# S5's VectorE work behind both RWKV inverses, an uninterrupted substitution, and the inverse's small products in turn through four quadrants

## The chip, the cores and the metric

The kernel runs on one core of a Trainium2 chip. The metric is the device time of one execution in microseconds. A core has a matrix engine (TensorE, PE in the profile; its weight loads are listed apart as PEld), VectorE (DVE), ScalarE (ACT) and GpSimd (POOL), and SyncE (SP), which here mostly issues DMAs. Each engine works through its own queue in order and waits on semaphores for the others.

## What is computed

Two layers act on 256 latent and 256 context tokens of width 1024. In each layer a gated feed-forward half step is followed by three token mixers on one normalised input, a merge through per-channel gates, and a second feed-forward half step. Cut to the part that matters:

```python
def hybrid_mixer(h, hc, need_ctx_out, w_in, ...):
    proj = h @ w_in; proj_c = hc @ w_in          # u | k | v | f (RWKV) | q | gate columns
    y_s5, y_s5_c = s5_mixer(u_c, u_l, ...)        # complex scans over tokens, both directions, then GELU and a gate
    y_att, y_att_c = gqa_mixer(q_c, k_c, v_c, q_l, k_l, v_l, ...)   # 8 query heads, 2 key heads of 64
    y_rw, y_rw_c = rwkv7_mixer(f_c, f_l, ...)     # 4 heads of 64, both directions
    g_s5, g_att, g_rw = jnp.split(jax.nn.sigmoid(gate_pre), 3, axis=-1)
    mixed = g_s5*(y_s5 @ w_br_s5) + g_att*(y_att @ w_br_att) + g_rw*(y_rw @ w_br_rwkv)
    return mixed @ w_out

def rwkv7_scan(s0, decay, neg_kk, kk_a, v, k, r):   # one step for each token
    sa = einsum(s, nkk_t)
    s = s*w_t + sa*b_t + v_t*k_t
    y = einsum(s, r_t)
```

The last layer gives no output for the context.

## The kernel before

All matmuls of the projections are split into a high and a low part of the weights (`wsplit`, ScalarE copies, VectorE or GpSimd subtracts: tiles gh.. and gl.., wh and wl) and run as three products (L922 to L924). In `mixers` (L1245) the projections come first; then RWKV, S5, attention and the merge share the rest of the stage. The gate projection (24 column blocks, tiles pg) depends on nothing in the mixers, and stands wherever TensorE would otherwise have nothing to do.

RWKV's token recurrence is worked off in chunks of 64 tokens, 4 chunks for each half of 256 tokens (`hf`=0 context, `hf`=1 latent), two directions, four heads. `head` and `piece` (L168 to L222) prepare a half: VectorE builds decayed keys and queries, TensorE multiplies them (tile it, L208), and VectorE masks the results into AM and ZL (L213, L214). Each chunk then needs the inverse of a unit triangular 64x64 matrix. `solve_a` writes the four 16x16 diagonal blocks of all 16 matrices through DRAM (Ad, L233) into a layout with matrices on partitions (G, L235), and inverts them by forward substitution on VectorE: 15 steps of one product (L240) and one sum (L241). The result goes through DRAM back (Sd, L242; D, L246). `solve_b` completes the inverse from 16 to 32 and then to 64: a transposition T (L252) and four batches of small products, pv (L256, 64 products on 16 rows), pS (L261, 64 on 32 rows), pw (L268, 32) and pT (L275, 32). Each product uses one quadrant of the 128 x 128 array, and a batch finishes one quadrant before it starts on the next. `loop` (L279) then carries the state through the chunks.

S5 (`s5_main`, L659 to L738) runs eight group-direction blocks: a product (tile s5v), VectorE products (L687, L688), scans (L694) and a product (L700), GpSimd sums between them, and a product back (tile s5y, L705 and L710). Its end is GELU and a gate (L723 to L737). Attention's pool is opened after S5's is closed and takes its memory, so attention begins (atz, L768, on GpSimd) when S5 is through. An attention unit (`core`, L838; four units in layer 0, two in layer 1) takes 256 or 512 keys: the scores' maxima (tile ats, L849), and then for each of two head groups and each 128 keys a step of three products (tile atp, L869 to L871), Exp on ScalarE (L873, tile atP, one buffer), a copy (L875, atph), a subtraction on VectorE (L876, atpl) and three products (tile ato, L878 to L880). A reciprocal (L884), a product (L885) and a split (L1278, L1279) end a unit. The merge follows: pb..e for S5 and RWKV, pb for attention.

The order of instructions on every engine is set by a scheduler when the kernel is built: it runs its own estimate of each engine's timeline and takes, among what is ready, the instruction written first, where `high_priority` moves a block ahead. `issue_after(i)` is a rule for that scheduler: what the block puts on the engine of instruction i stays behind i in that engine's queue. It is no wait by itself. `Rwkv.run` sets the sequence in which all of this is written:

```python
h0=s.head(0,0); h1=s.head(0,1); s.prep(h0)
between()
s.prep(h1); s.solve_a(0)
h0=s.head(1,0); h1=s.head(1,1); s.prep(h0)
s.solve_b(0); s.prep(h1); s.solve_a(1)
```

Of the kernel before, what the change touches and what calls it, by code (L numbers as in the profile page):

```python
# [52 lines left out]
class Rwkv:  # L53
# [170 lines left out]
    def solve_a(s,hf):  # L224

        K=s.K; nc=K.nc; L=s.L; V=nc.vector; ac=(0,64); nm=f"{L}{hf}"
        Ad=K.dram.tile([64,2,16,64],F32,name=f"Ad{nm}",tag="Ad",bufs=2)
        Sd=K.dram.tile([4,2,16,16,16],F32,name=f"Sd{nm}",tag="Sd",bufs=2)
        AMv=s.AM[:,hf].rearrange("p a c n -> p (a c) n")
        G=s.g1([128,16,16],f"G{nm}"); S=s.g1([128,16,16],f"S{nm}"); s.D=s.g2([128,16,32],f"D{nm}")  # L230
        nc.gpsimd.memset(S,0.0); nc.gpsimd.memset(S.rearrange('p a b -> p (a b)')[:,0:256:17],1.0); nc.gpsimd.memset(s.D,0.0)
        for par in range(2):
            nc.sync.dma_start(Ad[:,par],AMv[par*64:par*64+64,:,ac[par]:ac[par]+64])  # L233
        for b in range(4):
            nc.sync.dma_start(G[b*32:b*32+32],Ad[b*16:b*16+16,:,:,b*16:b*16+16].rearrange("i r s t -> (r s) i t"))  # L235
        tmp=K.rw.tile([128,64],F32,name=f"stmp{nm}",tag="stmp",bufs=1)
        for j in range(15):
            a=j+1; b=15-j
            tv=tmp[:,0:a*b].rearrange("p (a b) -> p a b",a=a)
            V.tensor_mul(tv,S[:,0:a,j:j+1].to_broadcast([128,a,b]),G[:,j:j+1,j+1:16].to_broadcast([128,a,b]))  # L240
            V.tensor_add(S[:,0:a,j+1:16],S[:,0:a,j+1:16],tv)  # L241
        nc.sync.dma_start(Sd.rearrange("b r s i t -> (b r s) i t"),S)  # L242
        for par in range(2):
            for b in range(4):
                r=par*64+b*16
                nc.sync.dma_start(s.D[r:r+16,:,b%2*16:b%2*16+16],Sd[b,par].rearrange("s i t -> i s t"))  # L246

    def solve_b(s,hf):

        K=s.K; nc=K.nc; L=s.L; V=nc.vector; ac=(0,64); nm=f"{L}{hf}"  # L250
        AMv=s.AM[:,hf].rearrange("p a c n -> p (a c) n"); D=s.D
        T=s.g2([128,16,32],f"T0{nm}"); V.transpose(T,D)  # L252
        pv=K.pc([128,16,32],f"pv{nm}")
        for g in range(4):
            R=slice(g*32,g*32+32); H=slice(g*32,g*32+16); c=ac[g//2]+g%2*32
            for m in range(16): h=nc.tensor.matmul(pv[R,m,:],AMv[H,m,c:c+32],T[H,m,:],start=True,stop=True)  # L256
        s.hops.append(h); VT=T; nc.scalar.activation(VT,pv,AF.Copy,scale=K.half[:,1:2])
        pS=K.pc([128,16,32],f"pS{nm}")
        for g in range(4):
            R=slice(g*32,g*32+32)  # L260
            for m in range(16): h=nc.tensor.matmul(pS[R,m,:],VT[R,m,:],D[R,m,:],start=True,stop=True)  # L261
        s.hops.append(h)
        V.tensor_add(D,D,pS)
        V.transpose(T,D)
        pv=K.pc([128,16,32],f"pw{nm}")
        for par in range(2):
            R=slice(par*64,par*64+32); R2=slice(par*64+32,par*64+64); a0=ac[par]
            for m in range(16): h=nc.tensor.matmul(pv[R2,m,:],AMv[R,m,a0+32:a0+64],T[R,m,:],start=True,stop=True)  # L268
            nc.scalar.activation(VT[R2],pv[R2],AF.Copy)
            nc.scalar.activation(AMv[R,:,a0:a0+32],D[R],AF.Copy)  # L270
            nc.scalar.activation(AMv[R2,:,a0+32:a0+64],D[R2],AF.Copy)
        s.hops.append(h); pS=K.pc([128,16,32],f"pT{nm}")
        for par in range(2):
            R=slice(par*64,par*64+32); R2=slice(par*64+32,par*64+64); a0=ac[par]
            for m in range(16): h=nc.tensor.matmul(pS[R,m,:],VT[R2,m,:],D[R2,m,:],start=True,stop=True)  # L275
            V.tensor_copy(AMv[R,:,a0+32:a0+64],pS[R])
        s.hops.append(h)

# [67 lines left out]
    def run(s,between):  # L346
        h0=s.head(0,0); h1=s.head(0,1); s.prep(h0)
        between()
        s.prep(h1); s.solve_a(0)
        h0=s.head(1,0); h1=s.head(1,1); s.prep(h0)  # L350
        s.solve_b(0); s.prep(h1); s.solve_a(1)
        l0=s.loop(0); l1=s.loop(1)
        for _ in range(3): next(l0)
        s.solve_b(1); next(l0); Y0=s.Y if not s.last else None
        for _ in range(4): next(l1)
        if not s.last: s.finish(0,Y0)
        s.finish(1,s.Y)
# [541 lines left out]
D=1024; NF=22; DEPTH=2  # L899
# [343 lines left out]
def ix(v,L): return v[L] if isinstance(v,tuple) else v['v']  # L1243

def mixers(tc,K,L,last):  # L1245
    nc=K.nc; I=K.I; n0=256 if last else 0
# [11 lines left out]
    with tc.tile_pool(name="mc",bufs=1) as mc, tc.tile_pool(name="q0",bufs=1) as q0, tc.tile_pool(name="prm",bufs=1) as K.prm, \  # L1258
# [24 lines left out]
        rw=Rwkv(K,L,W,last); rw.emit=lambda hf,o: ysplit(6,8,o) if last else nc.sync.dma_start(K.yd[:,6:8,hf*256:hf*256+256],o)  # L1283
# [46 lines left out]
        def between():  # L1330
            for o in K.SEQ[b+1:]: op(o)
        rw.run(between)
        with tc.tile_pool(name="s5",bufs=1) as sp, tc.high_priority(offset=ix(K.HS,L)):
            for _ in s5_main(K,L,sp,lambda m,o: ysplit(m,m+1,o.unsqueeze(1)) if last else nc.sync.dma_start(K.yd[:,m],o),last): pass
        N=512-n0; T=lambda sh,n,tag,b,dt=F32: K.rw.tile(sh,dt,name=f"{n}{L}",tag=tag,bufs=b)
        if not last: ay=T([128,2,4,512],"ay","BT",1,F32R)
# [116 lines left out]
```

## Time and profile before

| | |
|---|---|
| median of three runs | 2347.73 us (2344.19 to 2353.74) |
| profiled execution | 2359.33 us, span 2357.6 us |
| mean granted TensorE clock | 0.953 of full speed |
| busy: PE / PEld / DVE / ACT / POOL | 95 / 82 / 69 / 41 / 26% |
| mixers of layer 0, from RWKV's preparation to the end of the gates | 490 to 926 us |
| the same of layer 1 | 1778 to 2116 us |

The page gives shares over the whole span; stages with different limits are mixed in it. The views that cut the span into windows show the busy time of each engine and the granted clock for one stage. Matmuls are pipelined, so that records overlap: a single record lasts longer than the time until the next one starts, and the step of a row of equal matmuls is its length, less the tail of the last, divided by the number of steps.

### The profile page before, as it was taken

What the parts mean: (1) busy time and instruction counts of PE and PEld (TensorE: products, weight loads), DVE (VectorE), ACT (ScalarE), POOL (GpSimd) and SP (SyncE); (2) the same over time, 40 slices, a digit from 0 to 9 for tenths busy, and PEclk for the clock granted to TensorE, in tenths of its full rate; (3) what the DMA queues carried; (4) which work ended last, traced back from release to release, by engine and by line L of the source; (5) the groups of instructions that cost most, each with busy time, mean ns of one, the idle gap of its engine ahead of it and who ended that gap; (6) DMA issues with size and microseconds to landing.
All of it is one profiled execution on the core that took longest, in us unless ns stands there. A gap on an engine that the chain in (4) does not pass through costs nothing.

```text
span 2357.6 us, 40039 instructions
## 1 busy us (share of the span) xinstructions
PE 2242.8 (95%) x14438; PEld 1929.4 (82%) x14438; DVE 1623.2 (69%) x3202; ACT 973.7 (41%) x2005; POOL 607.1 (26%) x726
## 2 busy tenths in 40 slices
PE   7999889988999999899999999999999899998999
PEld 3888668866789889788888888888887688888999
DVE  7895889588855677886457575546557965687655
ACT  4333333433344544443233344334334325565554
POOL 5016660155422233600000002513013533331000
PEclk8999989998869999999999999999999877999999
DMA  7575566334422454545445436546424542365664
GB/s 254 165 225 171 182 214 219 121 119 144 123 82 76 138 163 143 185 141 184 123 143 182 126 131 206 171 155 215 138 65 131 150 126 85 94 194 184 178 188 130
DMA packets 222715, 363.40 MB, mean 154 GB/s; under 512 B 53554, under 2 KB 93618, under 8 KB 222388
## 3 DMA queue, kind: packets, MB, share of 16 engines
q1 hardware_dynamic: 220500, 360.09, 48.3%
q8 instruction: 113, 1.85, 0.3%
q10 hardware_dynamic: 2016, 0.76, 0.1%
q14 instruction: 86, 0.70, 0.1%
HBM read 320.90 MB, written 39.86 MB: 153 GB/s over the span
## 4 chain that ended last, share of the span: by engine, by line
PE 79%; DVE 10%; issue 4%; DMA 3%; POOL 2%; ACT 1%; SPq 1%; DVEq 0%; ACTq 0%; POOLq 0%
PE p L922 17%; PE p L924 17%; PE p L923 16%; PE pg L924 3%; PE pg L922 3%; PE pg L923 3%; DVE s L995 1%; PE pS L261 1%; PE pv L256 1%; PE pq L923 1%; PE po L922 1%; PE po L924 1%; PE po L923 1%; PE pq L922 1%; PE it L208 1%
## 5 line engine op out<-in xcount | busy, mean ns | idle before, releaser
L917 ACT ACTIVATE wh<-wr 128x512 fp32r<-128x512 f32 (+1 forms) x568 | 348.1, 619 | 666.3 <-PE p L923 578.1
L918 DVE TENSOR_TENSOR wl<-wr,wh 128x512 fp32r<-128x512 f32 (+1 forms) x568 | 407.3, 721 | 306.3 <-ACT wh L917 275.1
L922 PE MATMUL p<-hhi,wh 128*128 128x512 f32 (+1 forms) x1440 | 516.6, 363 | 4.7 <-ACT wh L917 3.6
L923 PE MATMUL p<-hlo,wh 128*128 128x512 f32 (+1 forms) x1440 | 518.6, 361 | 1.5 <-DVE hlo L1104 0.9
L924 PE MATMUL p<-hhi,wl 128*128 128x512 f32 (+1 forms) x1440 | 518.6, 361 | 0.6 <-DVE wl L918 0.6
L922 PEld LDWEIGHTS p<-hhi,wh 128*128 128x128 f32 x1440 | 273.2, 191 | 46.7 <-ACT wh L917 4.3
L923 PEld LDWEIGHTS p<-hlo,wh 128*128 128x128 f32 x1440 | 274.2, 190 | 42.9 <-DVE hlo L1104 1.8
L924 PEld LDWEIGHTS p<-hhi,wl 128*128 128x128 f32 x1440 | 274.0, 190 | 42.4 <-DVE wl L918 1.4
L995 DVE SCALAR_TENSOR_TENSOR s<-ad,cb 128x1024 f32<-128x1024 f32 x224 | 286.3, 1280 | 2.9
L924 PE MATMUL p<-ghi,wl 128*128 128x512 f32 (+1 forms) x704 | 248.3, 353 | 0.0
L922 PE MATMUL p<-ghi,wh 128*128 128x512 f32 (+1 forms) x704 | 248.0, 353 | 0.0
L923 PE MATMUL p<-glo,wh 128*128 128x512 f32 (+1 forms) x704 | 247.9, 353 | 0.0
L924 PE MATMUL pg<-hhi,glpg 128*128 128x256 f32 x512 | 157.9, 309 | 11.0 <-DVE glpg L907 9.0
L922 PE MATMUL pg<-hhi,ghpg 128*128 128x256 f32 x512 | 155.5, 304 | 0.3 <-ACT ghpg L906 0.3
L923 PE MATMUL pg<-hlo,ghpg 128*128 128x256 f32 x512 | 152.0, 297 | 0.0
L924 PEld LDWEIGHTS p<-ghi,wl 128*128 128x128 f32 x704 | 133.0, 189 | 18.2 <-issue 0.2
L923 PEld LDWEIGHTS p<-glo,wh 128*128 128x128 f32 x704 | 133.0, 189 | 18.1
L922 PEld LDWEIGHTS p<-ghi,wh 128*128 128x128 f32 x704 | 133.0, 189 | 17.9
L906 ACT ACTIVATE ghpg<-wrpg 128x256 fp32r<-128x256 f32 x176 | 72.3, 414 | 125.3 <-PE pg L923 102.9
L924 PEld LDWEIGHTS pg<-hhi,glpg 128*128 128x128 f32 x512 | 104.6, 205 | 18.8 <-DVE glpg L907 10.9
L907 POOL TENSOR_TENSOR glpg<-wrpg,ghpg 128x256 fp32r<-128x256 f32 x88 | 70.8, 808 | 180.8 <-ACT ghpg L906 168.7
L922 PEld LDWEIGHTS pg<-hhi,ghpg 128*128 128x128 f32 x512 | 104.8, 205 | 6.3 <-ACT ghpg L906 0.5
(722 smaller groups left out, 4325.5 us busy)
## 6 DMA issues: line engine op xcount, KB each, us to landing
wr<-w SPq DMA_DIRECT2D x480, 256.0 KB
ad<-w_ada SPq DMA_DIRECT2D x138, 512.0 KB
wrpg<-w_g SPq DMA_DIRECT2D x96, 256.0 KB
wr<-w SPq DMA_DIRECT2D x64, 192.0 KB
s5tab<-s5tabd SPq DMA_DIRECT2D x16, 640.0 KB
s5tabd<-s5tb SPq DMA_DIRECT2D x16, 384.0 KB
wrpf<-w_f SPq DMA_DIRECT2D x24, 256.0 KB
gd<-gt SPq DMA_DIRECT2D x24, 256.0 KB
```

What stands on the lines that cost most here:

```text
L208: nc.tensor.matmul(pi[:,c,:],BK[R,c].rearrange("p j b -> p (j b)"),s.ZL[par][R,hf,dq,c,o],start=True,stop=True)
L256: for m in range(16): h=nc.tensor.matmul(pv[R,m,:],AMv[H,m,c:c+32],T[H,m,:],start=True,stop=True)
L261: for m in range(16): h=nc.tensor.matmul(pS[R,m,:],VT[R,m,:],D[R,m,:],start=True,stop=True)
L906: K.nc.scalar.activation(hi,raw,AF.Copy)
L907: (K.nc.gpsimd if eng=='pool' else K.nc.vector).tensor_sub(lo,raw,hi.bitcast(F32))
L917: nc.scalar.activation(hi[:,0:n],raw,AF.Copy)
L918: (nc.gpsimd if eng=='pool' or i<=K.PW else nc.vector).tensor_sub(lo[:,0:n],raw,hi[:,0:n].bitcast(F32))
L922: nc.tensor.matmul(ps,lhi,rhi,start=start,stop=False)
L923: nc.tensor.matmul(ps,lhi,rlo,start=False,stop=False)
L924: return nc.tensor.matmul(ps,llo,rhi,start=False,stop=stop).ins
L995: nc.vector.scalar_tensor_tensor(j,raw,1.0,K.cb[:,v,:],op0=ALU.mult,op1=ALU.mult,accum_out=K.M[L][:,v,ct:ct+1])
```

## The change

It has three parts. `solve_a` remembers its last sum (`s.lasts`). After the first half's `solve_a`, one piece of the second half is written freely; the other one, the completion of the first inverse and the second direction's pieces are written under `issue_after(s.lasts)`: VectorE's rows of these come behind the whole first substitution. All of S5 is written under `issue_after(rw.after)`, the last sum of the second substitution. And the loops of the four product batches are exchanged: the matrix index is now the outer loop and the quadrant the inner one, so that successive products go to different quadrants (four of them in pv and pS, two in pw and pT); the copies behind pw get a loop of their own. No arithmetic is added or removed.

```diff
             V.tensor_mul(tv,S[:,0:a,j:j+1]...,G[:,j:j+1,j+1:16]...)
-            V.tensor_add(S[:,0:a,j+1:16],S[:,0:a,j+1:16],tv)
+            s.lasts=V.tensor_add(S[:,0:a,j+1:16],S[:,0:a,j+1:16],tv).ins
...
         pv=K.pc([128,16,32],f"pv{nm}")
-        for g in range(4):
-            R=slice(g*32,g*32+32); H=slice(g*32,g*32+16); c=ac[g//2]+g%2*32
-            for m in range(16): h=nc.tensor.matmul(pv[R,m,:],AMv[H,m,c:c+32],T[H,m,:],start=True,stop=True)
+        for m in range(16):
+            for g in range(4):
+                R=slice(g*32,g*32+32); H=slice(g*32,g*32+16); c=ac[g//2]+g%2*32
+                h=nc.tensor.matmul(pv[R,m,:],AMv[H,m,c:c+32],T[H,m,:],start=True,stop=True)
...
         pv=K.pc([128,16,32],f"pw{nm}")
+        for m in range(16):
+            for par in range(2):
+                R=slice(par*64,par*64+32); R2=slice(par*64+32,par*64+64); a0=ac[par]
+                h=nc.tensor.matmul(pv[R2,m,:],AMv[R,m,a0+32:a0+64],T[R,m,:],start=True,stop=True)
         for par in range(2):
             R=slice(par*64,par*64+32); R2=slice(par*64+32,par*64+64); a0=ac[par]
-            for m in range(16): h=nc.tensor.matmul(pv[R2,m,:],AMv[R,m,a0+32:a0+64],T[R,m,:],start=True,stop=True)
             nc.scalar.activation(VT[R2],pv[R2],AF.Copy)
...
-        h0=s.head(1,0); h1=s.head(1,1); s.prep(h0)
-        s.solve_b(0); s.prep(h1); s.solve_a(1)
+        h0=s.head(1,0); h1=s.head(1,1); s.piece(*h0[:2],0,h0[2][0],h0[3][0])
+        with s.K.tc.issue_after(s.lasts):
+            s.piece(*h0[:2],1,h0[2][1],h0[3][1])
+            s.solve_b(0); s.prep(h1)
+        s.solve_a(1); s.after=s.lasts
...
-        with tc.tile_pool(name="s5",bufs=1) as sp, tc.high_priority(offset=ix(K.HS,L)):
+        with tc.tile_pool(name="s5",bufs=1) as sp, tc.high_priority(offset=ix(K.HS,L)), tc.issue_after(rw.after):
```

pS and pT are turned round in the same way as pv and pw. The change adds 11 lines, all above S5, so that a line of S5, of attention or of the weight split has a number in the changed kernel that is 11 higher (L687 is L698, L880 is L891).

What the scheduler makes of it shows in three places. On VectorE in layer 0, at the first substitution (S, stmp and G are its tiles; th, T, ZL and BK belong to RWKV's preparation, s5.. to S5, and gl.. are split weights). Before:

```order
L240 TENSOR_TENSOR stmp_5684<-S_5673,G_5672 128x15
L169 SCALAR_TENSOR_TENSOR th_5742<-c_rst_4013,th_5742 128x256
L700 TENSOR_TENSOR s5qb_7230<-s5w_7223,s5tab_7209 128x4x127
L241 TENSOR_TENSOR S_5673<-S_5673,stmp_5684 128x15
L907 TENSOR_TENSOR glpg_4933<-wrpg_4930,ghpg_4932 128x256
L168 TENSOR_SCALAR th_5748<-th_5748 128x256
L240 TENSOR_TENSOR stmp_5684<-S_5673,G_5672 128x28
L169 SCALAR_TENSOR_TENSOR th_5748<-c_rst_4013,th_5748 128x256
L182 TENSOR_TENSOR T_5762<-k_4162,u_5754 128x256
L241 TENSOR_TENSOR S_5673<-S_5673,stmp_5684 128x2x14
L187 TENSOR_TENSOR ZL_4032<-kkn_4176,E_5756 64x4x64
```

and now:

```order
L240 TENSOR_TENSOR stmp_5684<-S_5673,G_5672 128x15
L918 TENSOR_TENSOR glkv_4916<-wrkv_4903,ghkv_4915 128x256
L241 TENSOR_TENSOR S_5673<-S_5673,stmp_5684 128x15
L240 TENSOR_TENSOR stmp_5684<-S_5673,G_5672 128x28
L241 TENSOR_TENSOR S_5673<-S_5673,stmp_5684 128x2x14
L918 TENSOR_TENSOR glpg_4933<-wrpg_4930,ghpg_4932 128x256
L240 TENSOR_TENSOR stmp_5684<-S_5673,G_5672 128x39
L241 TENSOR_TENSOR S_5673<-S_5673,stmp_5684 128x3x13
L240 TENSOR_TENSOR stmp_5684<-S_5673,G_5672 128x48
L918 TENSOR_TENSOR glpg_4949<-wrpg_4930,ghpg_4948 128x256
L241 TENSOR_TENSOR S_5673<-S_5673,stmp_5684 128x4x12
```

Between one product of the substitution and its sum stood pieces and S5 rows; now only splits of weights stand among the first steps. In the same queue, at the end of the second substitution of layer 0, before (att.. and at.. rows belong to attention's keys, glq to weights of its queries; S5's last row L737 stood some 50 rows earlier):

```order
L240 TENSOR_TENSOR stmp_6147<-S_6136,G_6135 128x28
L812 TENSOR_TENSOR atvl_7296<-atqw_7318,atvh_7295 128x2x64 x2
L241 TENSOR_TENSOR S_6136<-S_6136,stmp_6147 128x14x2
L791 TENSOR_REDUCE atss_7325<-atsqk_7324 128x4
L240 TENSOR_TENSOR stmp_6147<-S_6136,G_6135 128x15
L907 TENSOR_TENSOR glq_5344<-wrq_5331,ghq_5343 128x256
L792 TENSOR_SCALAR atss_7325<-atss_7325 128x4
L241 TENSOR_TENSOR S_6136<-S_6136,stmp_6147 128x15
```

and now:

```order
L241 TENSOR_TENSOR S_6136<-S_6136,stmp_6147 128x14x2
L325 COPY XV_6189<-p_6264 64x256
L240 TENSOR_TENSOR stmp_6147<-S_6136,G_6135 128x15
L241 TENSOR_TENSOR S_6136<-S_6136,stmp_6147 128x15
L698 TENSOR_TENSOR s5ra_6992<-s5v_6987,s5tab_6983 128x512
L699 TENSOR_TENSOR s5rb_6993<-s5v_6987,s5tab_6983 128x512
L918 TENSOR_TENSOR glq_5480<-wrq_5467,ghq_5479 128x256
```

S5's first VectorE row follows directly on the last sum; before, attention's preparation had come up to this place. On TensorE in layer 0, among the steps of attention's last unit (atq_, atk.., atm and atsel are its queries, keys and maxima, atph and atpl the two parts of the exponentials, pg gates). Before:

```order
L880 MATMUL ato_7865<-atpl_7873,atvh_7295 128x512
L922 MATMUL pg_9121<-hhi,ghpg_9158 128x256
L923 MATMUL pg_9121<-hlo,ghpg_9158 128x256
L924 MATMUL pg_9121<-hhi,glpg_9159 128x256
L922 MATMUL pg_9121<-hhi,ghpg_9158 128x256
L923 MATMUL pg_9121<-hlo,ghpg_9158 128x256
L869 MATMUL atp_7905<-atqs_7661,atkh_7293 128x512
L870 MATMUL atp_7905<-atqs_7661,atkl_7294 128x512
L871 MATMUL atp_7905<-atmT_7300,atsel_7305 128x512
```

and now:

```order
L889 MATMUL ato_7865<-atph_7872,atvh_7295 128x512
L890 MATMUL ato_7865<-atph_7872,atvl_7296 128x512
L891 MATMUL ato_7865<-atpl_7873,atvh_7295 128x512
L880 MATMUL atp_7905<-atqs_7661,atkh_7293 128x512
L881 MATMUL atp_7905<-atqs_7661,atkl_7294 128x512
L882 MATMUL atp_7905<-atmT_7300,atsel_7305 128x512
L889 MATMUL ato_7865<-atph_7885,atvh_7295 128x512
L890 MATMUL ato_7865<-atph_7885,atvl_7296 128x512
L891 MATMUL ato_7865<-atpl_7886,atvh_7295 128x512
```

Between the products of one step stood gate matmuls (and merge products of S5 and RWKV); now one step follows the other, and no gate is left behind them in this layer. In layer 1 it is the same for both units.

## Rows read from the trace of the kernel before

**Rows 1.** The page: PE's busy time, and the granted clock in 40 slices.

```profile
PE 2242.8 (95%) x14438; PEld 1929.4 (82%) x14438; DVE 1623.2 (69%) x3202; ACT 973.7 (41%) x2005; POOL 607.1 (26%) x726
...
PEclk8999989998869999999999999999999877999999
```

**Rows 2.** Busy time by stage, layer 0; columns as in the first line.

```profile
core 0: us, PE busy (x) PEld busy (x) DVE busy (x) ACT busy (x) POOL busy (x), PEclk, DMA share, GB/s
490.00:642.00 152.00, 130.41 (x769) 106.56 (x768) 135.34 (x264) 57.52 (x127) 81.00 (x101) 0.91 0.41 121
642.00:684.00 42.00, 42.00 (x435) 37.49 (x432) 16.47 (x52) 15.17 (x36) 8.12 (x11) 0.51 0.32 88
684.00:926.00 242.00, 241.66 (x2424) 220.52 (x2423) 156.79 (x311) 123.54 (x260) 69.49 (x71) 0.99 0.40 128
```

**Rows 3.** The same view of layer 1.

```profile
1778.00:1920.00 142.00, 120.59 (x744) 103.14 (x743) 124.50 (x263) 56.40 (x135) 64.63 (x91) 0.87 0.47 134
1920.00:2012.00 92.00, 90.69 (x1180) 80.85 (x1177) 46.20 (x105) 39.20 (x94) 29.69 (x37) 0.72 0.28 84
2012.00:2116.00 104.00, 99.58 (x893) 89.32 (x892) 76.61 (x145) 65.12 (x148) 31.57 (x37) 0.98 0.50 152
```

**Rows 4.** VectorE by line, 490 to 642 us (busy us, mean ns | idle before).

```profile
L694 DVE TENSOR_TENSOR_SCAN s5w<-s5m4m,s5ra 128x128 f32<-128x128 f32 x29 | 11.0, 431 | 1.1 <-POOL s5ra L689 1.1
...
L700 DVE TENSOR_TENSOR s5qb<-s5w,s5tab 128x508 f32<-128x508 f32 x8 | 5.9, 742 | 1.7 <-DMA Yd<-s5ysb 1.7
```

**Rows 5.** PE by line, 640 to 756 us: the four product batches.

```profile
L261 PE MATMUL pS<-D,T 32*32 32x32 f32 x256 | 11.5, 215 | 0.0
L256 PE MATMUL pv<-T,AM 16*32 16x32 f32 x256 | 10.9, 208 | 0.8 <-DVE T L252 0.8
L268 PE MATMUL pw<-T,AM 32*32 32x32 f32 x128 | 6.4, 214 | 0.0
L275 PE MATMUL pT<-D,T 32*32 32x32 f32 x128 | 5.9, 203 | 0.0
```

**Rows 6.** The largest of them in layer 1, 1915 to 2012 us.

```profile
L261 PE MATMUL pS<-D,T 32*32 32x32 f32 x256 | 14.2, 237 | 0.0
```

**Rows 7.** PE in order of time (start us, us); last: only 687.20 to 687.21 us.

```profile
724.02 3.93 PE L256 MATMUL pv<-T,AM 16*32 16x32 f32 x128
...
644.22 1.22 PE L256 MATMUL pv<-T,AM 16*32 16x32 f32 x19
...
690.52 0.68 PE L315 MATMUL p<-Z,AM 64*64 64x64 f32 x14
...
687.19 0.69 PE L295 MATMUL p<-XV,ZL 128*64 128x64 f32 x16
...
687.19 0.28 PE L295 MATMUL p<-XV,ZL 128*64 128x64 f32 x2
```

**Rows 8.** Who waited for S5's output tile s5o (us, times).

```profile
  POOL atz L768: 35.2, 2
```

**Rows 9.** PE by line, 904 to 926 us.

```profile
L923 PE MATMUL pg<-hlo,wppg 128*128 128x256 f32 x55 | 15.4, 279 | 0.0
```

**Rows 10.** ScalarE in order of time; last: all Exps of 2076 to 2102 us.

```profile
811.21 0.60 ACT L873 ACTIVATE atP<-atp 128x512 f32<-128x512 f32 x1 [0.51 <-PE atp L871]
811.84 0.63 ACT L875 ACTIVATE atph<-atP 128x512 fp32r<-128x512 f32 x1
...
813.24 0.60 ACT L873 ACTIVATE atP<-atp 128x512 f32<-128x512 f32 x1 [0.45 <-DVE atpl L876]
...
L873 ACT ACTIVATE atP<-atp x8: 578/588/604, 2077.1 to 2101.2; 128x512 f32<-128x512 f32 x8
```

**Rows 11.** VectorE in order of time, 899 to 912 us.

```profile
899.94 0.69 DVE L876 TENSOR_TENSOR atpl<-atP,atph 128x512 fp32r<-128x512 f32 x1 [1.98 <-ACT atph L875]
905.05 3.35 DVE L884 RECIPROCAL atdn<-atdn 128x512 f32<-128x512 f32 x1 [4.42 <-ACT atdn L883]
...
911.13 0.69 DVE L1279 TENSOR_TENSOR ay<-aty,ay 128x512 fp32r<-128x512 f32 x1 [0.58 <-ACT ay L1278]
```

More of the change, by code (lines that the diff above doesn't have):

```diff
@@ L253, in solve_b @@
         pv=K.pc([128,16,32],f"pv{nm}")
-        for g in range(4):
-            R=slice(g*32,g*32+32); H=slice(g*32,g*32+16); c=ac[g//2]+g%2*32
-            for m in range(16): h=nc.tensor.matmul(pv[R,m,:],AMv[H,m,c:c+32],T[H,m,:],start=True,stop=True)
+        for m in range(16):
+            for g in range(4):
+                R=slice(g*32,g*32+32); H=slice(g*32,g*32+16); c=ac[g//2]+g%2*32
+                h=nc.tensor.matmul(pv[R,m,:],AMv[H,m,c:c+32],T[H,m,:],start=True,stop=True)
         s.hops.append(h); VT=T; nc.scalar.activation(VT,pv,AF.Copy,scale=K.half[:,1:2])
         pS=K.pc([128,16,32],f"pS{nm}")
-        for g in range(4):
-            R=slice(g*32,g*32+32)
-            for m in range(16): h=nc.tensor.matmul(pS[R,m,:],VT[R,m,:],D[R,m,:],start=True,stop=True)
+        for m in range(16):
+            for g in range(4):
+                R=slice(g*32,g*32+32)
+                h=nc.tensor.matmul(pS[R,m,:],VT[R,m,:],D[R,m,:],start=True,stop=True)
         s.hops.append(h)
@@ L265, in solve_b @@
         pv=K.pc([128,16,32],f"pw{nm}")
+        for m in range(16):
+            for par in range(2):
+                R=slice(par*64,par*64+32); R2=slice(par*64+32,par*64+64); a0=ac[par]
+                h=nc.tensor.matmul(pv[R2,m,:],AMv[R,m,a0+32:a0+64],T[R,m,:],start=True,stop=True)
         for par in range(2):
             R=slice(par*64,par*64+32); R2=slice(par*64+32,par*64+64); a0=ac[par]
[L268 removed]
             nc.scalar.activation(VT[R2],pv[R2],AF.Copy)
@@ L272, in solve_b @@
         s.hops.append(h); pS=K.pc([128,16,32],f"pT{nm}")
+        for m in range(16):
+            for par in range(2):
+                R=slice(par*64,par*64+32); R2=slice(par*64+32,par*64+64)
+                h=nc.tensor.matmul(pS[R,m,:],VT[R2,m,:],D[R2,m,:],start=True,stop=True)
         for par in range(2):
-            R=slice(par*64,par*64+32); R2=slice(par*64+32,par*64+64); a0=ac[par]
-            for m in range(16): h=nc.tensor.matmul(pS[R,m,:],VT[R2,m,:],D[R2,m,:],start=True,stop=True)
+            R=slice(par*64,par*64+32); a0=ac[par]
             V.tensor_copy(AMv[R,:,a0+32:a0+64],pS[R])
```

## The prediction, made before the changed kernel was run

> **What bounds the kernel now.** I read the page first: TensorE is busy over nearly the whole span [rows 1]. A shorter time must therefore come out of the gaps of TensorE, out of stretches in which its clock is granted at the lower of its two levels (1.2 instead of 2.4 GHz), or out of matmuls that occupy it without need. The slices of the granted clock dip twice, in both layers inside the mixers, so I cut the mixers into stages [rows 2, 3]. Before the RWKV inverse can start ("preparation", 490 to 642 us in layer 0, 1778 to 1920 us in layer 1) TensorE works 130.4 of 152.0 us and 120.6 of 142.0 us. That is 21.6 and 21.4 us of idling, with VectorE busy for 135.3 and 124.5 us of it: VectorE is the engine that is full there. In the stage of the inverses TensorE hardly idles, but the clock is low: 0.51 of full speed over 42 us in layer 0, 0.72 over 92 us in layer 1. Up to the end of attention there is no slack worth naming: 0.3 us of 242 in layer 0, 4.4 us of 104 in layer 1. So the same work could gain in the preparation, in the clock, and in the small products of the inverse. Whatever empties the stage behind them can lose.
>
> **S5 out of the preparation.** By adding up, along VectorE's order, the traced durations of all rows from the first one that differs to the first transposition T of the inverse, 134 us of work stand ahead of T in layer 0 before the change, and 86 us after it (116 and 77 us in layer 1). S5's rows are 34 us of the 134, the scans (11.0 us in this stage) and the products of L700 (5.9) the largest groups [rows 4]; the other 14 are rows that the planner now puts behind T. TensorE has 93 us of work ahead of T in the new order of layer 0, so now the two engines are nearly level, and TensorE is the later one. Of the 21 us of idling I let 9 go in each layer. The bounds are 0 (the chain from one VectorE row to a product and back stays as long as it is) and 21 (all of it). Most of it stays because the substitution has a wait that the change leaves alone: the matrix goes through DRAM to be re-laid. S5's own matmuls are not removed; they are done later, where TensorE had no gap, and so the gap that they filled counts against the 21. S5's DMAs move too: in SP's order the later five of the eight tables and all its writes now stand behind the second substitution's transfers. That frees the substitution's transfers of them, and costs S5 nothing that TensorE sees as long as gate matmuls are left to run. **Sum: −9 and −9.**
>
> **The small products.** Per layer two inverses issue 768 records (384 products, two records each). The busy times of these four groups in layer 0 add to 11.5 + 10.9 + 6.4 + 5.9 = 34.7 us [rows 5]; in layer 1 the largest is 14.2 us and the four make 37.0 [rows 6]. Of one quadrant 128 records took 3.93 us; without the 0.19 us that the last outlives the others, 127 steps make 29.5 ns each at the full clock. At the lower clock 19 took 1.22 us, some 54 ns a step. The row that shows a turn between two quadrants is the loop's L295: its weights have 64 columns, twice as many, and 16 records still take only 0.69 us, some 31 ns each; of these, two had already started in the first 20 ns [rows 7]. So a turn through two quadrants halves the price, and I take that for pw and pT (12.3 to 6 us). Four in turn are not shown. Between the half that two give and the quarter that a perfect overlap would give I take a third for pv and pS: 22.4 to 8 us in layer 0, 25.2 to 9 in layer 1. **Sum: −20 and −22.** Bounds: all at half, −17 and −18; pv and pS at a quarter, −23 and −25; nothing at all, if four quadrants wait for each other. The separate loop of copies behind pw starts the first copies some 16 products later, under half a microsecond per inverse, which other matmuls cover.
>
> The Trainium skill, TensorE: Matmul & The Clock Gate, section "Wait — 56ns, not 53.3ns?", says that starts of matmuls never come closer than about 25 ns, however small they are. By that alone the 768 records would keep 19 us a layer, the gain would be some 27 us in place of 42, and the sum below 15 us higher. The row of L295 speaks against it: two of its records started within 20 ns [rows 7].
>
> **The clock.** In 642 to 684 us half of 42 us is lost, 20.6 us; in layer 1's stretch 0.28 of 92, 25.8 us [rows 2, 3]. Both spells follow a stretch in which TensorE waited, and consist of the small products. With fewer gaps ahead and shorter products some of it must return, but the products still fill only a corner of the array. I take **−8 and −8**, with bounds 0 and −21 and −26 (all of it).
>
> **What is late next: attention.** Attention's first instruction waits for the memory that S5 releases (atz, 35.2 us over the two layers) [rows 8]; S5 ended near 628 us in layer 0, and now can only begin behind the second substitution. TensorE has gate matmuls for that time, but they are the same ones that used to fill attention's steps. In TensorE's new order none is left for the last two attention units of either layer: their steps stand there bare. Before, attention's last result was followed by 22 us of gates in layer 0, of which the last kind alone, 55 of each of three, is 15.4 us a group [rows 9]; they hid everything at its end.
>
> A bare step of one head and 128 keys is a ring: Exp 0.60 us, copy 0.63 us (ScalarE), subtraction 0.69 us (VectorE), and only then the next Exp, since the tile between has one buffer: the Exp waits for atpl. The closest two Exps lie 813.24 − 811.21 = 2.03 us apart [rows 10]. I take 2.1 us. Two units are 16 steps: 34 us. Each unit's entry and drain (transposing the maxima, first Exp, the last step's six matmuls) I estimate at 5 us from the same durations, 10 us; behind the last step come two copies, the reciprocal of 3.35 us, the product, and the split that ends at 911.82, some 8 us from 903.8 [rows 10, 11]. Together 52 us. TensorE's work in it: six 512-wide products a step. In 904 to 926 us 191 products of 256 took 22 us, 0.115 us each, so a step has 1.4 us and 16 have 22; with the scores, transpositions and the few merge products in between some 29. So about 23 us of TensorE stand idle where layer 0 had none: +24 with the clock still full, and +20 in layer 1, which had 4.4 us of such idling [rows 3]. For the clock that may fall in these gaps I add 3 each. **Sum: +27 and +23.** Bounds: at 1.9 us a step (the three durations alone, 1.92) 6 us less in all; at the 3.4 us of layer 1's mean (24.1 us for 7 steps, [rows 10]) 42 us more.
>
> **How the numbers follow.** Layer 0: −9 −20 −8 +27 = −10. Layer 1: −9 −22 −8 +23 = −16. Together −26 us. The profiled execution took 2359.3 us (span 2357.6), 11.6 us above the median of the three runs, 2347.7. The sum goes on the first as 2333 and on the median as **2322 us**, 1.1% less. Half a percent (12 us) is about what a measurement of this kernel can tell from no change.
>
> **Rivals.**
> *The low clock goes away altogether.* If the spells are there because the long runs of small products occupy so little of the array, then shorter runs among full matmuls end them: 20.6 + 25.8 − 16 = 30 us more, 2292 us. For it: the clock is low just where these runs are, and nearly full (0.99) behind them. Against: half of layer 1's spell is beside such full matmuls already. Chance 0.2.
> *The preparation does not shorten.* VectorE's load falls, but the wait through DRAM and TensorE's own 93 us hold the inverse where it was: the 9 + 9 us do not come, 2340 us, and no difference that can be told. Products at half price in all four groups lie near it (2329). Chance 0.2, for products that save less in another way included.
> *Bare attention costs more than the rest brings* (the other side). It decides by one number, the time of a bare step: the 26 us are used up when 32 steps take 0.8 us more, at 2.9 us. With layer 1's mean of 3.4 us it is +42: 2364 us. For it: each step crosses PE, ScalarE, VectorE and PE, VectorE and ScalarE have other work to do in between, and only the closest pairs show 2.0. Against: the mean stems from steps that stood in a queue behind gate matmuls. Chance 0.12.
> *The products do not overlap at all through four quadrants*, so that the turn does nothing: +42, 2364 us. The Trainium skill, TensorEngine Tiling (Array Packing), "Gotcha 1: PSUM Pressure", says that different row tiles cannot access one PSUM bank at the same time, which is what pv's four quadrants would do. L295 does not decide it, since its two quadrants differ in columns alone; L315 speaks against it: its weights are 64x64, two row tiles write one tile of PSUM in turn, and 14 records take 0.68 us, some 35 ns a step [rows 7], where 64 columns of one quadrant would need about twice the 29.5. No row shows four. Chance 0.06.
> The forecast itself, 2308 to 2336 us, has 0.42.
>
> Faster by over half a percent (below 2336): 0.42 + 0.2 less what of the forecast's edge spills over, 0.60. Within: 0.22. Slower: 0.18. The range takes in the low-clock rival with 8 us to spare below, and above it ends at 2358, leaving out most of the two cases at 2364: 2284 to 2358.
>
> **What would show it.** The first T of layer 0 near 595 us in place of 641 and of layer 1 near 1880; a batch of 64 products in about 1 us; S5's last row near 730 us; gates used up near 857 us; behind that Exps 2.1 us apart with TensorE idle 0.7 us of each; TensorE's idle time in the preparation at 12 us a layer. I am wrong if bare steps are over 2.9 us, if 64 products still take 1.9 us, or if the granted clock over the stage of the inverses is what it was; the first two make it slower, the last costs 16 us. Right in sign but too small, if that clock is at 0.95.

## The result, and the profile after

The changed kernel takes 2382.5 us (median of four runs, 2374.7 to 2386.8) against 2350.7 us for the kernel before on the same chips: ratio 1.0118, 95% interval 1.0089 to 1.0147. It is slower by 1.2%, where 1.1% less was forecast. The profiled execution has a span of 2385.0 us, 27.4 more than before: layer 0's output projection ends 10 us later (1016.3 against 1006.3 us of the span), and layer 1 takes 18 us more.

The windows below are the stages of the forecast with the borders that the changed kernel has (T of the first inverse begins at 590 and 1890 us, the last gate ends at 869 and 2082, attention at 944 and 2146). The columns are those of [rows 2]; layer 0 first, then layer 1.

```profile
490.00:591.00 101.00, 88.50 (x499) 71.90 (x499) 81.85 (x166) 44.31 (x100) 39.27 (x64) 0.92 0.28 81
591.00:869.00 278.00, 264.88 (x3002) 239.74 (x3001) 184.49 (x360) 121.34 (x268) 107.92 (x113) 0.99 0.50 157
869.00:944.00 75.00, 52.76 (x157) 31.00 (x156) 40.31 (x58) 31.03 (x54) 2.74 (x7) 0.80 0.13 43
...
1786.00:1890.00 104.00, 88.72 (x527) 72.96 (x526) 78.36 (x172) 49.45 (x118) 35.88 (x60) 0.92 0.37 107
1890.00:2081.00 191.00, 168.92 (x2155) 150.29 (x2156) 136.53 (x298) 84.76 (x210) 87.79 (x103) 0.90 0.56 167
2081.00:2146.00 65.00, 46.17 (x155) 27.84 (x156) 33.82 (x51) 28.52 (x51) 2.62 (x2) 0.87 0.06 19
```

TensorE's idle time is the length of a window less its busy time. The preparation idles 12.5 and 15.3 us, where [rows 2, 3] had 21.6 and 21.4. The middle, from the inverse to the last gate, idles 13.1 and 22.1 us, where before there were next to none (0.3 in layer 0; 1.3 in layer 1 up to attention). Attention's bare end idles 22.2 and 18.8 us, where layer 1 had 4.4. In all that is 104 us against 49: 55 more, where the forecast had 26 (−9 −9 +24 +20).

The same work is done with less TensorE time all the same, and that is the products. TensorE by line, 590 to 700 us, which answers to [rows 5]:

```profile
L257 PE MATMUL pv<-T,AM 16*32 16x32 f32 x256 | 4.7, 198 | 0.0
L263 PE MATMUL pS<-D,T 32*32 32x32 f32 x256 | 3.8, 194 | 0.0
L281 PE MATMUL pT<-D,T 32*32 32x32 f32 x128 | 2.8, 192 | 0.2 <-ACT T L274 0.2
L271 PE MATMUL pw<-T,AM 32*32 32x32 f32 x128 | 2.4, 192 | 0.0
```

The four groups have gone from 34.7 to 13.7 us, in layer 1 from 37.0 to 14.8 (4.6 + 4.0 + 3.6 + 2.6): −21 and −22, the forecast's −20 and −22. So the part of the change that was costed from two quadrants is right; most of what went wrong lies in the idling.

### The profile page after: what moved, and what is told of

Same layout as the page of the kernel before. It is cut to its first block, busy times and chain, and to the rows that moved or that the text cites. A ratio compares the mean times of both kernels' runs of the same rounds, so it can differ in the third digit from the quotient of the medians.

```text
span 2385.0 us, 40057 instructions
## 1 busy us (share of the span) xinstructions
PE 2218.4 (93%) x14438; PEld 1878.4 (79%) x14438; DVE 1617.8 (68%) x3202; ACT 974.8 (41%) x2005; POOL 595.3 (25%) x726
## 4 chain that ended last, share of the span: by engine, by line
PE 72%; DVE 12%; DMA 4%; issue 4%; ACT 3%; POOL 2%; SPq 1%; DVEq 0%; ACTq 0%; POOLq 0%
PE p L935 16%; PE p L934 16%; PE p L933 16%; PE pg L935 2%; PE pg L933 2%; PE pg L934 2%; DVE s L1006 1%; PE it L208 1%; PE po L935 1%; DVE atpl L887 1%; PE po L933 1%; ACT atph L886 1%; PE po L934 1%; ACT atP L884 1%; PE pf L933 1%
## 5 line engine op out<-in xcount | busy, mean ns | idle before, releaser
L933 PEld LDWEIGHTS p<-ghi,wh 128*128 128x128 f32 x704 | 133.0, 189 | 18.1
L935 PEld LDWEIGHTS p<-ghi,wl 128*128 128x128 f32 x704 | 133.0, 189 | 18.1 <-issue 0.2
L934 PEld LDWEIGHTS pg<-hlo,ghpg 128*128 128x128 f32 x512 | 101.8, 199 | 1.0 <-issue 0.2
```

Of the source, the lines that this page charges most:

```text
L933: nc.tensor.matmul(ps,lhi,rhi,start=start,stop=False)
L934: nc.tensor.matmul(ps,lhi,rlo,start=False,stop=False)
L935: return nc.tensor.matmul(ps,llo,rhi,start=False,stop=stop).ins
```

## Experiments

All times of before in this section are those of the runs beside each kernel (2351 to 2355 us). S5's end is the end of the last row of its output s5o, attention's start the first score product (ats), both in layer 1 and counted from the end of layer 0's output projection, so that what layer 0 did is taken out; the layer's length is counted from there to the end of layer 1's output projection. These three columns come from one profiled execution of each kernel.

| kernel | median us | ratio to before, 95% | S5's end | attention starts | layer 1 |
|---|---|---|---|---|---|
| before | 2350.7 | | 949 | 1003 | 1151 |
| the change | 2382.5 | 1.0118 [1.0089, 1.0147] | 1016 | 1060 | 1169 |
| products_only | 2306.5 | 0.9809 [0.9787, 0.9831] | 936 | 980 | 1122 |
| subst_only | 2376.0 | 1.0107 [1.0064, 1.0149] | 974 | 1022 | 1164 |
| s5_only | 2417.2 | 1.0283 [1.0247, 1.0318] | 1021 | 1066 | 1179 |
| subst_products | 2337.6 | 0.9936 [0.9912, 0.9961] | 961 | 1002 | 1144 |
| s5_products | 2376.9 | 1.0089 [1.0066, 1.0111] | 1000 | 1042 | 1159 |
| after_hold | 2398.2 | 1.0186 [1.0156, 1.0217] | 1012 | 1050 | 1171 |
| subst_prod_L0 | 2308.9 | 0.9814 [0.9776, 0.9853] | 937 | 976 | 1124 |
| prod_s5sub1 | 2350.2 | 0.9989 [0.9963, 1.0014] | 986 | 1027 | 1158 |
| prod_two | 2302.5 | 0.9775 [0.9743, 0.9806] | 935 | 977 | 1119 |
| prod_hs6000 | 2315.5 | 0.9849 [0.9812, 0.9886] | 927 | 985 | 1131 |

### The three parts, one by one

The first four runs take the change apart, to tell three theories from each other that their expectations state: A (S5's late rows use up the gates ahead of attention), B (the products' saving is lost wherever it is made) and C (the held-up pieces of RWKV lose the time). products_only exchanges the loops of `solve_b` and nothing else:

```diff
-        for g in range(4):
-            ...
-            for m in range(16): h=nc.tensor.matmul(pv[R,m,:],...)
+        for m in range(16):
+            for g in range(4):
+                h=nc.tensor.matmul(pv[R,m,:],...)
```

> Only the loops of the four product batches are exchanged; S5 and the sequence in which RWKV is written stay as before. Theory A (S5 behind the inverses uses up the gates before attention, and its bare steps and the stage ahead of them cost some 65 us, while the products save what was forecast): the batches fall from 66 us of TensorE over both layers to about 21, some of the low clock returns, and gates still fill attention; 2295 to 2315 us. Theory B (the products are beside other waits, so their saving is lost wherever it is made): 2340 to 2352 us. Theory C (the held-up pieces of RWKV lose the time, not S5): as A, 2295 to 2315.

2306.5 us, 47 less than before: the range of theories A and C, theory B is out. The clock is nearly full where the products stood. The windows of this kernel from the first T to the last gate in layer 0, and from T to attention's end in layer 1:

```profile
636.00:901.00 265.00, 261.07 (x2882) 234.34 (x2881) 181.82 (x404) 139.35 (x297) 77.20 (x83) 0.97 0.43 134
...
1892.00:2058.00 166.00, 155.22 (x2033) 135.93 (x2033) 114.89 (x245) 98.79 (x234) 55.33 (x69) 0.96 0.43 133
```

The granted clock is 0.97 and 0.96 here; [rows 2, 3] had 0.51 and then 0.99, and in layer 1 0.72 and then 0.98.

subst_only takes the new sequence of `run` alone:

```diff
-        h0=s.head(1,0); h1=s.head(1,1); s.prep(h0)
-        s.solve_b(0); s.prep(h1); s.solve_a(1)
+        h0=s.head(1,0); h1=s.head(1,1); s.piece(*h0[:2],0,h0[2][0],h0[3][0])
+        with s.K.tc.issue_after(s.lasts):
+            s.piece(*h0[:2],1,h0[2][1],h0[3][1])
+            s.solve_b(0); s.prep(h1)
+        s.solve_a(1)
```

> Only the sequence of RWKV changes: one piece of the second half is written freely, and the completion of the first inverse and the other pieces have their VectorE rows behind the first substitution. Products one quadrant at a time, S5 unrestrained. Theory A: the inverse starts some 10 to 20 us earlier but the later pieces give most of it back, 2338 to 2352 us, with gates left behind attention's end in layer 0. Theory B: the same. Theory C (pieces held behind the substitution leave the second inverse late): 2370 us or more.

2376.0 us, 23 more than before. Theory A had none of that; theory C's bound is met.

s5_only takes S5's rule alone:

```diff
-        s.solve_b(0); s.prep(h1); s.solve_a(1)
+        s.solve_b(0); s.prep(h1); s.solve_a(1); s.after=s.lasts
...
-        with tc.tile_pool(name="s5",bufs=1) as sp, tc.high_priority(offset=ix(K.HS,L)):
+        with tc.tile_pool(name="s5",bufs=1) as sp, tc.high_priority(offset=ix(K.HS,L)), tc.issue_after(rw.after):
```

> Only S5's VectorE rows are put behind the second substitution; the sequence of RWKV and the products as before. Theory A: attention's last two units of both layers bare, TensorE's idle time at their steps as in the whole change, 2400 to 2425 us (the whole change without its saving in products). Theory B: about the whole change, 2375 to 2390 us, since products brought nothing there. Theory C: 2340 to 2355 us.

2417.2 us, 64 more: theory A's range, and against B and C as the main cause. This is the largest term of the whole change.

subst_products is the changed kernel without this rule:

> The whole change without the rule on S5: substitution in a row and products in turn, S5 between them as before. Theory A: gates fill attention again, products save, 2285 to 2310 us, under 2320 in any case. Theory B: 2340 to 2352 us. Theory C: 2330 us or more, well above the kernel with the products alone.

2337.6 us. S5's rule taken away returns 45 us (43 by the ratios to before), but the kernel stays 31 us above the products alone, where theory A had at most 14. (Its nine runs spread from 2328.9 to 2344.3 us, and the profiled one is the lowest, so its profile shows 21 of these 31 us.) So theory A holds for S5 and falls for the sequence: there are two losses, and the sequence's needs a cause.

### Where the sequence loses

The table shows it: in layer 0 subst_products and products_only end their output projection alike (982.0 and 983.0 us of the span), in layer 1 S5 ends 24 us later with the sequence, attention starts 22 later, and the layer is 22 longer. S5 itself is not slower on VectorE; its state is complete at 1883 us in subst_products (901 us after layer 0's end; 906 with the products alone). What is late is its way back through TensorE. GpSimd's last row of S5's last block, and, on ScalarE, the copy of that block's product out of TensorE (start us, us, engine, line):

```profile
1882.06 0.68 POOL L712 TENSOR_TENSOR s5S<-s5S,s5qb 128x256 f32<-128x256 f32 x1
...
1916.25 0.28 ACT L723 ACTIVATE s5ysb<-s5y 128x128 f32<-128x128 f32 x1
```

Between them lie 34 us, in which TensorE works through gates, RWKV's products and the batch pS of the inverse; S5's last products stand among and behind these rows in its queue. With the products alone only 5 us lie between the same two rows:

```profile
1888.49 0.68 POOL L709 TENSOR_TENSOR s5S<-s5S,s5qb 128x256 f32<-128x256 f32 x1
...
1894.19 0.28 ACT L720 ACTIVATE s5ysb<-s5y 128x128 f32<-128x128 f32 x1 [3.10 <-PE s5y L718]
```

Attention cannot start until S5's end is through. The theory that takes A's and C's place is E: a layer pays for every microsecond by which S5's end, and with it attention's start, comes later, as far as there are no gates left to lay over the rest.

One rival is left that no run separates from this. From the first T to the first score product of layer 1 the granted clock was 0.78 in subst_products and 0.90 with the products alone:

```profile
1870.60:1984.30 113.70, 98.94 (x1371) 84.17 (x1371) 63.61 (x157) 47.83 (x117) 38.16 (x48) 0.78 0.35 97
```

```profile
1891.60:1962.80 71.20, 62.75 (x1183) 54.88 (x1184) 45.26 (x110) 37.98 (x93) 25.54 (x33) 0.90 0.38 113
```

That is 25 and 7 us of clock lost, and the difference is nearly the 22 us that layer 1 is longer. Which of the two, the place in the queue or the clock, makes the other is not shown.

subst_prod_L0 tests theory E by leaving the rule away in layer 1:

```diff
-        with s.K.tc.issue_after(s.lasts):
+        with s.K.tc.issue_after(s.lasts) if s.L==0 else nullcontext():
```

> Products in turn in both layers, RWKV's new sequence with its rule in layer 0 alone, S5 unrestrained. Theory E (a layer pays only where S5's end comes later and with it attention's start): in layer 0 S5's end does not move and gates are left over, so nothing is paid, 2298 to 2312 us, the time of the products alone. Theory C (holding RWKV's pieces back costs about the same in each layer): half of the 31 us between the products alone and the products with the sequence, 2317 to 2327 us.

2308.9 us: nothing that can be told is paid in layer 0; the loss was layer 1's. Theory C is out. (One thing that is different in layer 1 is that a gate block has 24 matmuls of 256 columns there, since the context needs no gates, and 48 in layer 0: 576 against 1152 in all.)

### Is it the idling at the bare steps, or the late start?

after_hold is the changed kernel, with some of the last gates kept back for attention:

```diff
-        gates(16-ng[0])
+        n=16-ng[0]; gates(max(0,n-HOLD[L]))
+        with tc.issue_after(marks[-2]): gates(min(n,HOLD[L]))
```

(HOLD is 3 in layer 0 and 4 in layer 1; marks holds each unit's last score product.)

> The whole change, and of the gates that are written behind attention the last 3 blocks of layer 0 and the last 4 of layer 1 are put, on TensorE, behind the scores' maxima of the last unit but one: attention's last two units get about as many gate matmuls between their steps as before the change (439 and 294 against 414 and 364). Theory D (TensorE's idling at the bare steps is itself the loss, as in the prediction): some 45 us come back, 2325 to 2345 us. Theory E (S5's late end, and with it attention's late start, is the loss; the idling only shows where there is nothing left to do, and steps with gates between them are longer): the idling moves ahead of attention and its steps grow, 2375 to 2405 us.

2398.2 us, 16 more than the changed kernel, in theory E's range and 53 above the upper end that theory D has. In layer 1 the steps are filled, and it helps nothing: from the first score product to the last step TensorE idles 1.7 us in place of 14.7, but from T to that product 38.3 in place of 21.8, and the layer is no shorter (1171 us, 1169). The gates are too few for both places, and filled steps take longer (first score product to the last step of layer 1: 64 us bare, 75 with the gates kept back, 97 before). So in layer 1 the idling behind the last gate is where the late start shows, not what it costs. Layer 0 does not test this: there the same stretch idles 21.5 us with the gates kept back and 19.0 without.

prod_s5sub1 gives half the dose, S5 behind the first substitution:

```diff
-        s.prep(h1); s.solve_a(0)
+        s.prep(h1); s.solve_a(0); s.after1=s.lasts
...
-        with tc.tile_pool(name="s5",bufs=1) as sp, tc.high_priority(offset=ix(K.HS,L)):
+        with tc.tile_pool(name="s5",bufs=1) as sp, tc.high_priority(offset=ix(K.HS,L)), tc.issue_after(rw.after1):
```

> Products in turn, RWKV's sequence as before, S5's VectorE rows behind the first substitution instead of the second: half the delay. In TensorE's order attention's last two units keep some fill (177 and 196 gate and merge matmuls instead of 451 and 350, and 18 to 46 behind the second). Theory E: S5 ends 30 to 50 us later than with the products alone, attention starts as much later, and gates pay back about half of it: 2330 to 2350 us, between 2306 and 2377. A threshold (no cost while any fill is left): 2300 to 2315.

2350.2 us, just above theory E's range (by 0.2); a threshold for both layers together is out. s5_products completes the series (products in turn, S5 behind the second substitution, RWKV's sequence as before):

> S5 behind the second substitution and products in turn, RWKV's sequence as before the change. If the parts add (S5 alone +64, products alone -47): 2370 us, and the substitution's sequence then costs about 12 us more in the whole change (2382). If S5's rule hides the cost of the substitution's sequence, because S5 waits for the second substitution, which that sequence brings sooner or later: below 2365 us would say that the sequence costs even there, above 2390 us that it helps there.

2376.9 us against 2370 by plain addition, and 6 below the whole change, with intervals that overlap: the parts nearly add, and where S5 waits for the second substitution the sequence costs little more. In the kernels with products in turn layer 1 takes 1119, 1122, 1124, 1144, 1158, 1159, 1171 and 1169 us where S5 ends at 935, 936, 937, 961, 986, 1000, 1012 and 1016: 81 us later make 50 us more. In the same order the clock lost from T to the layer's end (the window's length times what its granted clock lacks of 1) is 4, 7, 7, 31, 22, 26, 44 and 29 us, so this series does not hold the clock still. The pair of subst_products and the whole change does, in layer 1: they lose 31 and 29 us there, and layer 1 is still 25 us longer with S5's rule.

Layer 0, which the table leaves out, pays for S5's rule too, and in another shape. With the products alone, with S5 behind the first substitution and with S5 behind the second, S5 ends at 626, 709 and 745 us of the span and layer 0 at 983, 990 and 1017: the first 83 us cost 7, the next 36 cost 27. In layer 1 the same two steps cost 36 and 1 us (1122, 1158, 1159). In the whole change layer 0 ends 34 us later than in subst_products (1016 against 982), so that about half of what S5's rule costs is paid there (34 of 59 us by these two profiles; up to 16 of the 34 are clock lost behind T, 24 against 8).

### The other direction, and a turn through two

prod_s5first writes S5's block ahead of RWKV's. In layer 1 S5's result is put into the space of the normalised context; written there so early, it replaces data that later projections read, so that part of layer 1 is computed from other data, and these projections wait for S5.

```diff
+        with tc.tile_pool(name="s5",bufs=1) as sp, ...: for _ in s5_main(...): pass
         rw.run(between)
-        with tc.tile_pool(name="s5",bufs=1) as sp, ...: for _ in s5_main(...): pass
```

> The reverse of the change's second part: products in turn, RWKV's sequence as before, and S5 written ahead of RWKV, so that VectorE takes S5's rows first. Theory E: S5 ends earlier in layer 1, where little else holds attention, and the layer ends earlier by a part of that: 2280 to 2300 us. Theory D: gates filled attention already with the products alone, so nothing is won: 2300 to 2312 us. A third possibility, that RWKV's preparation and with it the inverse come too late: 2315 us or more.

2346.3 us, by number the third possibility. Because of those waits it says nothing on theory E. prod_hs6000 asks the same with a priority:

```diff
-K.HS=(0,0)
+K.HS=(6000,6000)
```

> Products in turn, everything else as before, but S5's block gets a higher priority in the scheduler (an offset of 6000 for both layers instead of 0), so that S5's last VectorE rows stand some 10 to 30 rows earlier. Theory E: S5's end moves forward by about 5 to 15 us and layer 1 gains up to as much: 2292 to 2306 us. Without a gain from an earlier S5: 2303 to 2312.

2315.5 us: a miss for both. S5 ended 10 us earlier in layer 1 (927 against 936), and yet attention started 6 us later and the inverse's first T 14 us later (1908.5 − 985.8 = 923 us after layer 0's end; with the products alone 1891.6 − 983.0 = 909). So an earlier end of S5 is not passed on, and theory E is one-sided. That VectorE's other work is the reason does not show: between S5's end and the first score product it works 32.9 of 58.8 us here, and 32.0 of 43.4 with the products alone. What the trace has there is more work on TensorE (51.6 us against 38.0), a granted clock of 0.85 against 0.92, and a wait of GpSimd for attention's table atrope of 7.5 us against 1.9.

prod_two takes pv and pS through two quadrants at a time:

```diff
-        for m in range(16):
-            for g in range(4):
+        for gp in range(2):
+          for m in range(16):
+            for g in (gp*2,gp*2+1):
```

> The kernel with the products alone in turn, but pv and pS go through two quadrants at a time (0 and 1, then 2 and 3) instead of four. If four quadrants overlap in full, an uninterrupted batch of 128 records takes about 2.1 us here (15 ns a step) and 1.3 us with four (8.5 ns); 512 records a layer make 3 us, so 2305 to 2318 us in all. If two already reach a floor, both take the same, and the time is that of the products alone, 2300 to 2312 us.

An uninterrupted batch of 128 records in products_only, and then in prod_two:

```profile
712.49 1.29 PE L257 MATMUL pv<-T,AM 16*32 16x32 f32 x128
```

```profile
704.51 2.12 PE L258 MATMUL pv<-T,AM 16*32 16x32 f32 x128
```

With the last record's 0.19 us taken off, 127 steps make 8.7 ns with four, 15.2 with two, and 29.5 with one [rows 7]: the overlap is nearly complete (half and a quarter of 29.5 are 14.8 and 7.4). The whole kernel takes 2302.5 us (two runs), in the range given for a floor and under the other one; the batches themselves rule the floor out, and the last halving, 3 us a layer by the expectation, is worth nothing that can be told in the whole.

## Why the prediction was wrong

**The products**: right. −20 and −22 forecast, −21 and −22 measured, by the third that was taken between a half and a quarter (pv and pS together 22.4 to 8.5 us in layer 0, 8.2 in layer 1). The rival that they do not overlap (chance 0.06) is out. So is the floor of about 25 ns between starts that was weighed in the prediction (the Trainium skill, TensorE: Matmul & The Clock Gate, "Wait — 56ns, not 53.3ns?"): the batch above has 8.7. (The prediction's working of that floor was off: 768 records at the page's 25 ns are 19.2 us a layer, an estimate; of 34.7 and 37.0 that leaves a gain of 33 us in place of 42 and a sum 9 higher, not 27 and 15.) Neither does the Trainium skill, TensorEngine Tiling (Array Packing), "Gotcha 1: PSUM Pressure", hold here: four row tiles write different partitions of one tile of PSUM in turn, at the same 8.7 ns.

**The preparation**: right where it was looked at, and lost behind. The first T came at 590 and 1890 us (595 and 1880 forecast), the idling fell by 9.1 and 6.1 us (9 and 9).

**"That ... costs S5 nothing that TensorE sees as long as gate matmuls are left to run"**: this is the step that failed. Between T and the last gate TensorE idles 13.1 and 22.1 us where the forecast had nothing, and taking the rule on S5 away returns 45 us of the whole. RWKV's new sequence was given no price of its own either; it costs 23 us alone, 31 beside the products, and some 6 where S5 waits for the second substitution anyway. What TensorE waits for in layer 1 (1890 to 2081 us; us in total, times, longest):

```profile
PE gt L394 <- DVE Yrw L387: 4.8, 1, 4.8
PE pg L935 <- POOL glpg L918: 4.7, 7, 1.6
PE pg L935 <- DVE glpg L918: 2.8, 4, 0.9
PE p L323 <- DVE Z L305: 1.8, 1, 1.8
```

Gates were left, but for 7.5 of the 22.1 us the low part of their weights (glpg) was not there; the longest single wait, 4.8 us, is for RWKV's output. S5's work was not hidden by moving it; the stage it went to had to carry it: from T to attention's end of layer 1 VectorE works 170.4 us (136.5 + 33.8) over 256, with the products alone 114.9 over 166. Why the splits came late is open: VectorE is busy for 136.5 us of 191, and ahead of these very splits it waits 23.9 us for ScalarE's copies (ghpg).

**Attention's end**: the ring was right, the idling came out by luck, and the surroundings were mis-sized. Three Exps in a row of the last unit but one (columns as in [rows 10]):

```profile
898.61 0.60 ACT L884 ACTIVATE atP<-atp 128x512 f32<-128x512 f32 x1 [0.76 <-DVE atpl L887]
...
900.63 0.60 ACT L884 ACTIVATE atP<-atp 128x512 f32<-128x512 f32 x1 [0.76 <-DVE atpl L887]
...
902.65 0.60 ACT L884 ACTIVATE atP<-atp 128x512 f32<-128x512 f32 x1 [0.76 <-DVE atpl L887]
```

They are 2.02 us apart, waiting for atpl, as the ring says (2.1 taken; over a unit of eight the mean is 2.2); the rival that hung on 2.9 us did not come about, though its sign did. The idling came out as +22 and +14 us where +24 and +20 were forecast, but not where it was forecast. Layer 0 from the last gate on: the third unit's entry, its steps, the last unit's entry, its steps, the drain (columns of [rows 2]):

```profile
869.00:887.00 18.00, 8.30 (x21) 4.74 (x20) 14.01 (x22) 5.14 (x10) 2.54 (x2) 0.59 0.51 160
887.00:905.00 18.00, 16.59 (x54) 9.57 (x53) 7.79 (x12) 10.87 (x18) 0.00 (x0) 0.93 0.05 15
905.00:918.60 13.60, 8.49 (x26) 5.60 (x26) 8.13 (x12) 2.35 (x5) 0.00 (x0) 0.75 0.00 0
918.60:937.00 18.40, 15.38 (x51) 8.39 (x49) 5.54 (x8) 11.02 (x19) 0.00 (x0) 1.00 0.00 1
937.00:944.00 7.00, 4.00 (x9) 2.70 (x10) 4.84 (x5) 1.65 (x3) 0.20 (x5) 0.52 0.00 0
```

The sixteen bare steps hold 4.4 us of the idling, 0.2 and 0.4 us a step where 0.7 was forecast: a product with no other behind it counts as busy to its own end (0.39 us, where the next start behind it is 0.23 us away otherwise), and in the third unit scores of the last one stand between the steps. The other 17.8 us lie in the entries and the drain. These are also why the stretch lasts 75 and 65 us in place of 52. An entry and drain was taken at 5 us; the third unit's first Exp stands 18.1 us behind the last gate, and between the last step of the third unit and the first Exp of the last, ScalarE shows 12.7:

```profile
905.93 0.59 ACT L892 ACTIVATE aty<-ato 64x512 f32<-64x512 f32 x1 [2.02 <-PE ato L891]
...
912.85 0.63 ACT L1289 ACTIVATE ay<-aty 128x512 fp32r<-128x512 f32 x1 [5.71 <-DVE atmh L865]
918.60 0.60 ACT L884 ACTIVATE atP<-atp 128x512 f32<-128x512 f32 x1 [3.28 <-PE atp L882]
```

and VectorE why: the maxima that the next unit needs stand behind the reciprocal of the unit before it.

```profile
907.68 3.34 DVE L895 RECIPROCAL atdn<-atdn 128x512 f32<-128x512 f32 x1
910.94 1.22 DVE L862 TENSOR_REDUCE atm<-ats 128x1 f32<-128x512 f32 x2
912.08 0.68 DVE L896 TENSOR_TENSOR aty<-aty,atdn 128x512 f32<-128x512 f32 x1
912.68 0.16 DVE L865 CAST atmh<-atm 128x8 fp32r<-128x8 f32 x1
```

And the clock: 0.80 over 75 us and 0.87 over 65 lose 15 and 8 us, where 3 and 3 were added; a part of that falls on TensorE's idle time, where it costs nothing. The windows above have it at 0.59, 0.75 and 0.52 in the entries and the drain, where TensorE waited, and at 0.93 and 1.00 in the steps.

**The clock elsewhere**: rival "the low clock goes away altogether" was mostly right where the products alone were changed: by the windows' means, 0.03 of 265 and 0.04 of 166 us are lost (8 and 7 us) where 20.6 and 25.8 were. In the whole change 45 us are lost again by the windows of the first section: 15 and 8 in bare attention, 19 in layer 1's middle (0.10 of 191) and 3 in layer 0's.

**The sum.** Idling +55 (forecast +26), products −43 (−42); the span rose by 27. The remaining +15 is nearly all busy time: the page's busy time of TensorE fell by 24 only (2242.8 to 2218.4). Each record counted up to the next one's start, attention's products (ats, atp, ato) take 100 us where they took 79, the merge's pb 42 in place of 34, and pq, of which the lower level had 31 us before and has next to none now, 45 in place of 58. By layers the forecast had −10 and −16; the profiles have +10 and +18. The deeper fault is the question asked. Each stage was balanced by TensorE's idle time, as if work were interchangeable between stages. What the experiments point to is a chain, S5's end, attention's keys and queries, attention, merge. In layer 1 it had little slack, and the change put 67 us on it (949 to 1016); in layer 0 it had some 80 us by the runs above, and the change put 115 on it (630 to 746). The price was to be read from what waits for S5's last row, which [rows 8] showed: attention's first instruction. Range and chances were set around the bare step, the one number of that chain that was looked at.

What stays open: how the 45 us of S5's rule divide between the split weights in the middle, attention's entries, and the low clock (after_hold shows only that layer 1's share cannot be bought back by gates); whether the 22 us of the sequence in layer 1 are S5's place in TensorE's queue or the lower clock there; and why an earlier S5 does not bring attention forward in prod_hs6000, which no run tried by itself.

## What to carry to other kernels

Before a block is put behind another on one engine, follow its last row to whoever waits for it, and add up that chain to the end of the stage; filler on the bottleneck engine hides a delay only while there is filler, and while that filler is ready. A change that joins a good part and a bad one should be taken apart: here the loop exchange alone gives 2306.5 us (0.9809, interval 0.9787 to 0.9831), the best of what was found together with its two-quadrant form, and the two reorderings cost 64 and 23 us by themselves. Small products of a quadrant each belong in turns through the quadrants.

## What was not expected of the hardware

A turn through four quadrants overlaps nearly in full: 29.5, 15.2 and 8.7 ns a record for one, two and four, with four row tiles writing one PSUM tile. And with the loops exchanged the kernel's mean granted clock rose from 0.953 to 0.970, though the products' own array work is the same: the runs of one-quadrant products went with the low clock (0.51 over 42 us with TensorE never idle, [rows 2]).
